# Eight buffers for parts of weights, each moved by 32 bytes more than the one before

## The chip, the cores and the metric

The program runs on one core of one Trainium2 chip. The metric is the device time of one execution in microseconds. The core's engines are TensorE (PE in the profile; its weight loads have a row of their own, PEld), VectorE (DVE), ScalarE (ACT), GpSimd (POOL) and SyncE (SP, which here issues the transfers).

## The reference

The program computes two layers of a decoder trunk on 512 positions of width 1024, in float32. Layer one is a gated short convolution followed by a feed-forward block with a convolution and a SiLU gate (inner width 2816). Layer two is an attention with forget gates (16 heads of 64) whose keys and values come from one shared projection, followed by a second feed-forward block of the same shape. Every block begins with an RMS norm and ends with an addition to the residual stream. Nearly all of the arithmetic is in the weight products:

```
proj = xn @ w_in                         # 1024 x 3072
x = x + (b * causal_dwconv(c * h)) @ w_out
kvf = h @ w_kvf;  qg = xn @ b_w_qg       # 1024 x 2064, 1024 x 2048
up = xn @ w_up                           # 1024 x 5632, in both layers
x = x + (silu(causal_dwconv(a)) * g) @ w_down   # 2816 x 1024, in both layers
```

## The kernel before

The residual stream lies transposed in SBUF as eight tiles of 128 features x 512 positions. Each float32 operand of a product is split into two parts, a high part (rounded to the matmul's float32r format) and a low part (the rest), and a product is made of three matmuls: high by high, high by low, low by high. The helper mac (L124 to L132) issues these three for each half of the 512 positions, so six matmuls of 256 columns for one block of 128 x 128 weights. In the order of its lines, L130 and L131 hold the high part of the weights as the stationary operand, L132 the low part. The moving operand is a tile of 2048 bytes per partition, read from its start (first half) or from 1024 bytes behind it (second half).

The weights come from HBM by SP's queue into wraw, three buffers of 128 x 1024 float32. The helper weights (L114 to L122) takes each buffer in pieces of up to 512 columns, and parts (L106 to L112) makes the two parts of a piece: ScalarE copies it into a whi buffer (L110), VectorE subtracts that from the piece into a wlo buffer (L111). A buffer holds four blocks of weights, at 0, 512, 1024 and 1536 bytes. There are four whi and four wlo buffers, used in turn; a buffer is free again when the last matmul that reads it is done. In the projection of the values (L368 to L404) the same buffers are filled in the same way but are the moving operand, and the activations are the stationary one.

The program gives addresses to its pools in the order in which they are opened (L58 to L65): const, big (58 tiles named g, which hold the activations' parts among others), sp (10 tiles s), ptp, misc, small, wraw, and last wsp with whi and wlo. All tiles from big to misc are 2048 bytes per partition, those of small are nine of 64 bytes, those of wraw 4096. So a whi or wlo buffer begins 576 bytes (nine times 64) behind a multiple of 2048 bytes counted from any g or s tile, the same for all eight of them. The addresses stand in no row of the trace; they follow from the tiles' sizes. The program's order on each engine is set by the order of its text and by the dependencies between tiles; no planner's cost enters it.

```
wraw = ctx.enter_context(tc.tile_pool(name="wraw", bufs=3))
wsp = ctx.enter_context(tc.tile_pool(name="wsp", bufs=4))
```

Of the kernel before, what the change touches and what calls it, by code (L numbers as in the profile page):

```python
# [15 lines left out]
F32 = mybir.dt.float32  # L16
F32R = mybir.dt.float32r
# [6 lines left out]
P = 128  # L24
T = 512
# [28 lines left out]
def trunk(ctx: ExitStack, tc: tile.TileContext, x_t, a_in, a_out, up0, down0, wk, wv, wf, wqg, b_out,  # L54
# [7 lines left out]
    misc = ctx.enter_context(tc.tile_pool(name="misc", bufs=8))  # L62
    small = ctx.enter_context(tc.tile_pool(name="small", bufs=3))
    wraw = ctx.enter_context(tc.tile_pool(name="wraw", bufs=3))
    wsp = ctx.enter_context(tc.tile_pool(name="wsp", bufs=4))  # L65
    banks = {n: ctx.enter_context(tc.tile_pool(name=n, bufs=b, space=PSUM))
             for n, b in (("mm", 2), ("st", 4), ("at", 2))}
    dram = ctx.enter_context(tc.tile_pool(name="dram", bufs=1, space=DRAM))
# [3 lines left out]
    def new(pool, tag, shape, dtype, **kw):  # L72
        count[0] += 1
        return pool.tile(shape, dtype, tag=tag, name=f"{tag}_{count[0]}", **kw)

    def G(dtype=F32):
        return new(big, "g", [P, T], dtype)

    def M(dtype=F32):
        return new(misc, "m", [P, T], dtype)  # L80
# [3 lines left out]
    def bank(name):  # L84
        return new(banks[name], name, [P, T], F32)
# [7 lines left out]
    pr = const.tile([P, NPAR], F32, tag="pr", name="pr")  # L93
    cs = const.tile([P, C_ET], F32, tag="cs", name="cs")
    x = [G() for _ in range(KT)]
    ones = const.tile([P, P], F32R, tag="ones", name="ones")
    nc.vector.memset(ones.bitcast(F32), 1.0)
    busy = G(F32R)
    nc.vector.memset(busy.bitcast(F32), 0.0)
    idle = bank("at")  # L100
# [4 lines left out]

    def parts(raw, n):  # L106

        hi = new(wsp, "whi", [P, T], F32R)
        lo = new(wsp, "wlo", [P, T], F32R)
        nc.scalar.copy(out=hi[:, :n], in_=raw)  # L110
        nc.vector.tensor_tensor(out=lo[:, :n], in0=raw, in1=hi[:, :n].bitcast(F32), op=ALU.subtract)  # L111
        return [(hi[:, c:c + P], lo[:, c:c + P]) for c in range(0, n, P)]  # L112

    def weights(src, nk=KT):  # L114

        cuts = [0, 8] if nk == 8 else [0, 8, 15, 22]
        for c0, c1 in zip(cuts[:-1], cuts[1:]):
            raw = new(wraw, "wraw", [P, 1024], F32)
            nc.sync.dma_start(out=raw[:, :(c1 - c0) * P], in_=src[:, c0 * P:c1 * P])
            for c in range(0, c1 - c0, 4):  # L120
                n = min(4, c1 - c0 - c) * P
                yield from parts(raw[:, c * P:c * P + n], n)  # L122

    def mac(ps, lh, rh, first, last):  # L124

        for h in range(2):

            f = slice(h * T // 2, (h + 1) * T // 2)
            go, end = first and h == 0, last and h == 1
            nc.tensor.matmul(ps[:, f], lhsT=lh[0], rhs=rh[0][:, f], start=go, stop=False, skip_group_check=True)  # L130
            nc.tensor.matmul(ps[:, f], lhsT=lh[0], rhs=rh[1][:, f], start=False, stop=False, skip_group_check=True)  # L131
            nc.tensor.matmul(ps[:, f], lhsT=lh[1], rhs=rh[0][:, f], start=False, stop=end, skip_group_check=True)  # L132
# [26 lines left out]
    def split(src, hi=None, lo=None, eng=None):  # L159
        hi = hi if hi is not None else G(F32R)  # L160
        lo = lo if lo is not None else G(F32R)
        nc.scalar.copy(out=hi, in_=src)  # L162
        (eng or nc.vector).tensor_tensor(out=lo, in0=src, in1=hi.bitcast(F32), op=ALU.subtract)  # L163
        return hi, lo
# [165 lines left out]
    def attention(norm, nxt_norm):  # L330
# [37 lines left out]
        for half in range(2):  # L368
            pv = [bank(n) for n in (("mm", "mm", "st", "st"), ("st", "st", "mm", "mm"))[half]]
            for u in range(4):  # L370
                raw = new(wraw, "wraw", [P, 1024], F32)
                nc.sync.dma_start(out=raw, in_=wv[half, u])
                w = []
                for c in (0, T):
                    hi = new(wsp, "whi", [P, T], F32R)
                    lo = new(wsp, "wlo", [P, T], F32R)
                    nc.scalar.copy(out=hi, in_=raw[:, c:c + T])
                    nc.vector.tensor_tensor(out=lo, in0=raw[:, c:c + T], in1=hi.bitcast(F32), op=ALU.subtract)
                    w.append((hi, lo))

                def step(t, k2):
                    k = 2 * u + k2
                    q = slice(t * P, (t + 1) * P)
                    mac(pv[t], (xkv[k][0][:, q], xkv[k][1][:, q]), w[k2], k == 0, k == KT - 1)

                if u < 3:
                    for k2 in range(2):
                        for t in range(NB):
                            step(t, k2)
                    if half == 0 and u == 1:  # L390
                        r, v1 = norm.finish()
                    if half == 0 and u == 2:

                        rt = const.tile([P, 16], F32, tag="rt", name="rt")[:, 0:NB]
                        tp = bank("st")
                        for i in range(NB):
                            nc.tensor.transpose(out=tp[:, i * H:(i + 1) * H], in_=r[:H, i * P:(i + 1) * P],
                                                identity=ident[:H, :H])
                        nc.vector.tensor_copy(out=rt, in_=tp[:, 0:NB * H].rearrange("p (i h) -> p i h", h=H)[:, :, 0])
                else:  # L400
                    for t in range(NB):
                        for k2 in range(2):
                            step(t, k2)
            for t in range(NB):  # L404
                for e in range(2):
                    v = G(F32R)
                    vs[t].append(v)
                    v = v.rearrange("p (c s d) -> p c s d", s=2, d=HD)
                    src = pv[t][:, e * 256:e * 256 + 256].rearrange("p (c d) -> p c d", d=HD)
                    nc.scalar.activation(out=v[:, :, e], in_=src, func=AF.Copy, scale=rt[:, t:t + 1])  # L410
                    nc.vector.scalar_tensor_tensor(out=v[:, :, 1 - e], in0=src, scalar=rt[:, t:t + 1],
                                                   in1=v[:, :, e].bitcast(F32), op0=ALU.mult, op1=ALU.subtract)
# [394 lines left out]
    ffn(up0, down0, PC_F[0], n2, n3, spill=True)  # L807
    n4 = Norm("ffn1")
    attention(n3, n4)
    ffn(up1, down1, PC_F[1], n4, None, last=True)  # L810

# [67 lines left out]
```

## Time and profile before

| | |
|---|---|
| median of 2 runs | 1233.8 us (1231.85 to 1235.76) |
| the profiled execution | 1233.1 us, of it 1231.3 us from the first to the last instruction |
| TensorE matmuls | 1216.5 us busy, 99% of the span, 10425 instructions |
| TensorE weight loads | 1189.0 us, 97%, 10425 instructions |
| VectorE, ScalarE, GpSimd | 678.6, 537.4, 203.1 us (55%, 44%, 16%) |
| TensorE's granted clock, mean | 0.996 |
| transfers | 124.14 MB, mean 101 GB/s |

Matmuls are pipelined: the 276 ns shown for one of 256 columns is its way from start to end, and several are under way at once. What the stream of them costs is read from the distance between their starts, so from counts over a stretch of time, or from the first and the last start of an unbroken run.

### The profile page before, as it was taken

What the parts mean: (1) busy time and instruction counts of PE and PEld (TensorE: products, weight loads), DVE (VectorE), ACT (ScalarE), POOL (GpSimd) and SP (SyncE); (2) the same over time, 40 slices, a digit from 0 to 9 for tenths busy, and PEclk for the clock granted to TensorE, in tenths of its full rate; (3) what the DMA queues carried; (4) which work ended last, traced back from release to release, by engine and by line L of the source; (5) the groups of instructions that cost most, each with busy time, mean ns of one, the idle gap of its engine ahead of it and who ended that gap; (6) DMA issues with size and microseconds to landing.
All of it is one profiled execution on the core that took longest, in us unless ns stands there. A gap on an engine that the chain in (4) does not pass through costs nothing.

```text
span 1231.3 us, 24568 instructions
## 1 busy us (share of the span) xinstructions
PE 1216.5 (99%) x10425; PEld 1189.0 (97%) x10425; DVE 678.6 (55%) x1163; ACT 537.4 (44%) x973; POOL 203.1 (16%) x181
## 2 busy tenths in 40 slices
PE   9999999999999999999999899999999999999998
PEld 8999999999999999999998788889999999999998
DVE  6755556555555533344646787876565555553222
ACT  5433345334333433333556767775543334342221
POOL 0100021111111100000123435442111111110000
PEclk9999999999999999999999999999999999999999
DMA  6233233333333344342342212124233233233341
GB/s 215 87 103 101 88 104 92 97 104 93 97 104 91 93 130 125 121 140 87 95 139 79 84 52 86 53 87 129 86 104 101 89 103 101 89 99 104 116 119 45
DMA packets 39374, 124.14 MB, mean 101 GB/s; under 512 B 4384, under 2 KB 4896, under 8 KB 39264
## 3 DMA queue, kind: packets, MB, share of 16 engines
q1 hardware_dynamic: 38048, 120.41, 31.8%
q10 hardware_dynamic: 1152, 1.97, 0.5%
q8 instruction: 81, 1.33, 0.4%
q14 instruction: 29, 0.24, 0.1%
q0 software_dynamic: 64, 0.20, 0.0%
HBM read 118.33 MB, written 4.23 MB: 100 GB/s over the span
## 4 chain that ended last, share of the span: by engine, by line
PE 90%; ACT 4%; DVE 3%; POOL 2%; issue 1%; DMA 0%; SPq 0%; DVEq 0%; POOLq 0%; ACTq 0%
PE st L131 18%; PE st L130 17%; PE st L132 17%; PE mm L130 11%; PE mm L132 11%; PE mm L131 11%; ACT s L189 1%; PE st L620 1%; PE at L658 1%; PE st L649 1%; POOL m L667 1%; DVE s L624 1%; DVE wlo L111 1%; ACT g L189 1%; ACT g L162 1%
## 5 line engine op out<-in xcount | busy, mean ns | idle before, releaser
L130 PE MATMUL st<-g,whi 128*128 128x256 f32 x1686 | 465.5, 276 | 0.0
L131 PE MATMUL st<-g,whi 128*128 128x256 f32 x1686 | 465.4, 276 | 0.0
L132 PE MATMUL st<-g,wlo 128*128 128x256 f32 x1686 | 465.4, 276 | 0.0
L110 ACT CAST whi<-wraw 128x512 fp32r<-128x512 f32 (+1 forms) x394 | 240.4, 611 | 473.6 <-PE st L131 291.9
L111 DVE TENSOR_TENSOR wlo<-wraw,whi 128x512 fp32r<-128x512 f32 (+1 forms) x394 | 283.6, 720 | 222.9 <-ACT whi L110 218.3
L130 PE MATMUL mm<-g,whi 128*128 128x256 f32 x1242 | 346.2, 279 | 0.0
L131 PE MATMUL mm<-g,whi 128*128 128x256 f32 x1242 | 343.5, 277 | 0.0
L132 PE MATMUL mm<-g,wlo 128*128 128x256 f32 x1242 | 343.5, 277 | 0.0
L130 PEld LDWEIGHTS st<-g,whi 128*128 128x128 f32 x1686 | 316.6, 188 | 0.1
L131 PEld LDWEIGHTS st<-g,whi 128*128 128x128 f32 x1686 | 316.5, 188 | 0.1
L132 PEld LDWEIGHTS st<-g,wlo 128*128 128x128 f32 x1686 | 316.5, 188 | 0.0
L130 PEld LDWEIGHTS mm<-g,whi 128*128 128x128 f32 x1242 | 233.5, 188 | 1.8
L131 PEld LDWEIGHTS mm<-g,whi 128*128 128x128 f32 x1242 | 233.4, 188 | 1.3
L132 PEld LDWEIGHTS mm<-g,wlo 128*128 128x128 f32 x1242 | 233.2, 188 | 0.1
L323 POOL TENSOR_TENSOR m<-m,m 128x512 f32<-128x512 f32 x44 | 69.1, 1573 | 408.3 <-DVE m L322 370.9
L162 ACT CAST g<-m 128x512 fp32r<-128x512 f32 x66 | 40.8, 619 | 90.4 <-POOL m L323 66.8
L163 DVE TENSOR_TENSOR g<-m,g 128x512 fp32r<-128x512 f32 x51 | 36.8, 722 | 67.3 <-ACT g L162 66.7
L224 POOL TENSOR_TENSOR m<-m,m 128x512 f32<-128x512 f32 x21 | 27.9, 1330 | 175.5 <-ACT m L222 153.6
L640 POOL TENSOR_SCALAR s<-s,sm 128x128 f32<-128x128 f32 (+3 forms) x64 | 41.4, 660 | 75.5 <-DVE sm L637 69.2
L189 ACT ACTIVATE s<-s,bb 128x128 f32<-128x128 f32 (+3 forms) x64 | 35.4, 555 | 22.9 <-DVE bb L633 22.8
L241 ACT ACTIVATE m<-m,pr 128x512 f32<-128x512 f32 x52 | 37.7, 725 | 15.9 <-DVE m L316 13.0
L242 DVE SCALAR_TENSOR_TENSOR m<-m,pr,m 128x511 f32<-128x511 f32 x52 | 39.0, 750 | 9.5 <-ACT m L241 9.5
(170 smaller groups left out, 1312.3 us busy)
## 6 DMA issues: line engine op xcount, KB each, us to landing
wraw<-up SPq DMA_DIRECT2D x88, 512.0 KB, 3.5
wraw<-down SPq DMA_DIRECT2D x32, 448.0 KB, 3.5
wraw<-a_in SPq DMA_DIRECT2D x21, 512.0 KB, 3.6
wraw<-down SPq DMA_DIRECT2D x16, 512.0 KB, 3.5
wraw<-wqg SPq DMA_DIRECT2D x16, 512.0 KB, 3.6
wraw<-a_out SPq DMA_DIRECT2D x8, 512.0 KB, 3.5
ld<-xsp SPq DMA_DIRECT2D x16, 256.0 KB, 2.8
wraw<-wv SPq DMA_DIRECT2D x8, 512.0 KB, 3.6
```

The source lines that it names most:

```text
L110: nc.scalar.copy(out=hi[:, :n], in_=raw)
L111: nc.vector.tensor_tensor(out=lo[:, :n], in0=raw, in1=hi[:, :n].bitcast(F32), op=ALU.subtract)
L130: nc.tensor.matmul(ps[:, f], lhsT=lh[0], rhs=rh[0][:, f], start=go, stop=False, skip_group_check=True)
L131: nc.tensor.matmul(ps[:, f], lhsT=lh[0], rhs=rh[1][:, f], start=False, stop=False, skip_group_check=True)
L132: nc.tensor.matmul(ps[:, f], lhsT=lh[1], rhs=rh[0][:, f], start=False, stop=end, skip_group_check=True)
L162: nc.scalar.copy(out=hi, in_=src)
L163: (eng or nc.vector).tensor_tensor(out=lo, in0=src, in1=hi.bitcast(F32), op=ALU.subtract)
L189: chain["exp"] = ordered(nc.scalar.activation(**kw), chain["set"])
L241: nc.scalar.activation(out=y, in_=src, func=AF.Copy, scale=pr[:, col + 2:col + 3])
L242: nc.vector.scalar_tensor_tensor(out=y[:, 1:T], in0=src[:, 0:T - 1], scalar=pr[:, col + 1:col + 2], in1=y[:, 1:T], op0=ALU.mult, op1=ALU.add)
L323: nc.gpsimd.tensor_tensor(out=g, in0=g, in1=y, op=ALU.mult)
L640: nc.gpsimd.tensor_scalar(out=s, in0=s, scalar1=sm[:, e:e + 1], scalar2=1.0, op0=ALU.mult, op1=ALU.mult)
```

## The change

The pool wsp is replaced by two, whip for the four whi buffers and wlop for the four wlo buffers. Ahead of them a pool with one tile of 32 bytes per partition (pad0), which nothing writes or reads, is put behind wraw. Each buffer is allocated with 520 columns, 2080 bytes, of which the first 512 columns are used as before. A helper WP hands out a pair. Counted from a g tile, modulo 2048 bytes, the four whi buffers then begin at 608, 640, 672 and 704, the four wlo buffers at 736, 768, 800 and 832. The instructions and their order in the text are the same.

```diff
-    wsp = ctx.enter_context(tc.tile_pool(name="wsp", bufs=4))
+    ctx.enter_context(tc.tile_pool(name="pad0", bufs=1)).tile([P, 8], F32, tag="pad0", name="pad0")
+    whip = ctx.enter_context(tc.tile_pool(name="whip", bufs=4))
+    wlop = ctx.enter_context(tc.tile_pool(name="wlop", bufs=4))
...
+    def WP():
+
+        hi = new(whip, "whi", [P, T + 8], F32R)[:, 0:T]
+        return hi, new(wlop, "wlo", [P, T + 8], F32R)[:, 0:T]
...
     def parts(raw, n):
-        hi = new(wsp, "whi", [P, T], F32R)
-        lo = new(wsp, "wlo", [P, T], F32R)
+        hi, lo = WP()
...
                 for c in (0, T):
-                    hi = new(wsp, "whi", [P, T], F32R)
-                    lo = new(wsp, "wlo", [P, T], F32R)
+                    hi, lo = WP()
```

## Rows read from the trace of the kernel before

**Rows 1.** The page's part 1: TensorE's busy time, share, instructions.
```profile
PE 1216.5 (99%) x10425; PEld 1189.0 (97%) x10425; DVE 678.6 (55%) x1163; ACT 537.4 (44%) x973; POOL 203.1 (16%) x181
```

**Rows 2.** The page's part 4: the chain that ended last, by engine.
```profile
PE 90%; ACT 4%; DVE 3%; POOL 2%; issue 1%; DMA 0%; SPq 0%; DVEq 0%; POOLq 0%; ACTq 0%
```

**Rows 3.** Groups of instructions by line and shape: count, busy us, mean ns, idle before.
```profile
L130 PE MATMUL st<-g,whi 128*128 128x256 f32 x1686 | 465.5, 276 | 0.0
...
L130 PE MATMUL mm<-g,whi 128*128 128x256 f32 x1242 | 346.2, 279 | 0.0
...
L130 PE MATMUL st<-s,whi 128*128 128x256 f32 x110 | 30.4, 276 | 0.0
...
L130 PE MATMUL mm<-whi,g 128*128 128x256 f32 x64 | 18.1, 282 | 0.0
```

**Rows 4.** Waits of TensorE, two of ten rows: total us, times, longest.
```profile
PE st L620 <- DVE mx L624: 3.4, 1, 3.4
...
PE mm L130 <- ACT g L162: 0.6, 1, 0.6
```

**Rows 5.** Windows, TensorE alone: length, busy (count), granted clock, DMA share, GB/s.
```profile
33.00:193.00 160.00, 160.00 (x1414) 1.00 0.31 96
200.00:540.00 340.00, 340.00 (x3003) 1.00 0.35 105
...
840.00:1190.00 350.00, 350.00 (x3088) 1.00 0.35 105
```

**Rows 6.** Timeline of TensorE, first stage: start us, duration us, instruction.
```profile
13.06 0.28 PE L130 MATMUL mm<-g,g 128*128 128x256 f32 x1
...
25.54 0.28 PE L132 MATMUL st<-g,g 128*128 128x256 f32 x1
25.65 0.28 PE L130 MATMUL st<-g,whi 128*128 128x256 f32 x1
...
31.19 0.28 PE L132 MATMUL st<-g,wlo 128*128 128x256 f32 x1
```

**Rows 7.** Timeline of TensorE, the projection of the values.
```profile
543.61 0.28 PE L130 MATMUL mm<-whi,g 128*128 128x256 f32 x1
...
544.29 0.28 PE L130 MATMUL st<-whi,g 128*128 128x256 f32 x1
...
544.56 0.39 PE L130 MATMUL mm<-whi,g 128*128 128x256 f32 x1
...
545.02 0.28 PE L130 MATMUL mm<-whi,g 128*128 128x256 f32 x1
...
554.44 0.28 PE L131 MATMUL st<-wlo,g 128*128 128x256 f32 x1
```

**Rows 8.** Timeline of TensorE, the keys' projection.
```profile
593.66 0.28 PE L130 MATMUL mm<-g,whi 128*128 128x256 f32 x1
...
605.44 0.28 PE L131 MATMUL mm<-g,whi 128*128 128x256 f32 x1
...
609.20 0.28 PE L130 MATMUL mm<-g,whi 128*128 128x256 f32 x1
...
609.54 0.28 PE L130 MATMUL mm<-g,whi 128*128 128x256 f32 x1
```

**Rows 9.** Timeline of TensorE: two matmuls of 512 columns with 16 columns of weights.
```profile
623.73 0.39 PE L506 MATMUL at<-m,E 128*16 128x512 f32 x1
623.96 0.40 PE L507 MATMUL at<-m,E 128*16 128x512 f32 x1
```

**Rows 10.** Groups of ScalarE and VectorE: count, busy us, mean ns, idle before and releasers.
```profile
L111 DVE TENSOR_TENSOR wlo<-wraw,whi 128x512 fp32r<-128x512 f32 x362 | 265.9, 735 | 192.7 <-ACT whi L110 188.1 <-PE st L131 2.0 <-PE mm L131 2.0
...
L110 ACT CAST whi<-wraw 128x512 fp32r<-128x512 f32 x362 | 224.0, 620 | 418.8 <-PE st L131 254.8 <-PE mm L131 134.3 <-ACT m L222 10.6
...
L242 DVE SCALAR_TENSOR_TENSOR m<-m,pr,m 128x511 f32<-128x511 f32 x52 | 39.0, 750 | 9.5 <-ACT m L241 9.5
...
L169 DVE SCALAR_TENSOR_TENSOR g<-g,pr,g 128x512 fp32r<-128x512 f32 x32 | 23.6, 750 | 4.8 <-ACT g L168 4.7
```

## Prediction

> **What bounds the kernel now.** I read the engines' busy times first: TensorE fills 99% of the span [rows 1], and the chain of waits lies on it for 90% [rows 2]. The groups by line come next: matmuls that load a whi or wlo buffer as weights are, over L130, L131 and L132, 3 x (1686 + 1242 + 110) = 9,114 of 10,425, and those that stream one are 6 x 64 = 384 [rows 3]. The idle time ahead of them is nothing. TensorE's list of waits says the same from the other side: its longest wait is 3.4 us, once, in the attention, and among its ten rows none is for the copy or the subtraction that fills these buffers [rows 4]. So neither filling nor freeing the buffers sets the end; the distance from one matmul's start to the next does, and only through it can an address count.
>
> That distance is read from counts. In three long windows, which hold 7,505 matmuls, it is 113.2 to 113.3 ns, at a granted clock of 1.00 [rows 5]; at that level (2.4 GHz) 256 columns are 106.7 ns by themselves. But the same shape also runs at other distances. In the first stage, where weights and moving tiles are both g tiles, 104 steps take 12.48 us, 120.0 ns each; the next matmuls load whi and wlo, and with no pause between the two 47 steps take 5.54 us, 117.9 ns each [rows 6]. That is the one place where a change of buffer alone goes with a change of pace, so the profile doesn't rule out that addresses matter. Two other places show what else matters. The values' projection begins at 113.3 ns (six steps in 0.68 us), is held up once, and then runs at 117.8 ns (80 steps in 9.42 us) with the same kinds of operands at the same distances from each other [rows 7]. The keys' projection runs at 117.8 ns (100 steps in 11.78 us) with g and whi, and after a hold-up at 113.3 ns with the same two [rows 8]. So there are several paces, a hold-up can switch between them at equal addresses, and the fast one has most of the time.
>
> **The change part by part.** It adds no instruction and no wait. The tile of 32 bytes is never written or read. The pools ahead of it keep their addresses, so SP's transfers into wraw land where they did, in the same order. whi and wlo had four buffers each and still have, freed by the same last matmuls; one pool or two makes no difference to who waits for whom. All this is 0, and nothing covers it, because nothing is issued.
>
> The copies and subtractions write to, and partly read from, buffers that begin at odd multiples of 32 bytes. No copy of before writes to such a place. The nearest row is VectorE's work in the convolution, whose operands begin one column (4 bytes) off: 750 ns for 511 columns, the same as 750 ns for 512 columns that begin on a tile's start [rows 10]. I take 0. If each copy took twice its 620 ns, the idle time ahead of it, 418.8 us over 362 copies or 1.16 us each, nearly all of it waiting for TensorE to free a buffer, would hold the added 0.62 us; the subtraction, 735 ns, has 0.53 us of idle ahead of it [rows 10]. What would be late next, were that cover gone, is the matmul at the head of a new buffer; today none waits.
>
> What is left is the reading by TensorE. Before, every weight block stood 576 bytes, modulo 512 thus 64, from the moving tile's grid. After, the eight buffers stand at 96, 128, 160, 192 (high) and 224, 256, 288, 320 (low) modulo 512; four of the eight, one in two in each kind, are at an odd multiple of 32 bytes, which no operand of before is. Bounds: from above, every one of the 9,114 at the 120.0 ns of the g tiles [rows 3, 6], 9,114 x 6.7 = 61 us more. From below, every one at the bare 106.7 ns, 9,114 x 6.6 = 60 us less. In between, the stretches now at 117.8 with whi or wlo (48 in the first stage, some 101 in the keys, the 384 of the values) go to 113.3: 533 x 4.5 = 2.4 us less [rows 6 to 8].
>
> I take 0, by the long windows. They run through four blocks in each of eight buffers, and through both halves of the moving tile. Counted modulo 2048 the weights there lie 64, 576, 1088 and 1600 bytes from the moving tile, and the pace is the same to 0.1 ns over 340 us [rows 5]. The first six steps of the values, where the two operands change places (the distance is then minus 64), keep it too [rows 7]. And the 6.6 ns over the bare columns aren't the weights': two matmuls of 512 columns with 16 columns of weights start 0.23 us apart, about twice 113.3, where a load eight times smaller should have given most of the excess back [rows 9].
>
> The Trainium skill speaks here as well: "SBUF — State Buffer", section "Who interferes with whom", says that contention arises only at the port pair that VectorE and GpSimd share, and that TensorE waits for nobody at SBUF. By it the change is worth 0 whatever the offsets. The trace agrees in the long windows, but equal shapes at 113.3, 117.8 and 120.0 ns are something that the section doesn't explain, so I don't take it as proof.
>
> The sum is 0 against the profiled execution's own 1233.1 us (a span of 1231.3 and 1.8 around it), which lies 0.7 under the median of the two runs, 1233.8. I forecast 1233.5 us; this case by itself reaches from 1230.7 (the 2.4 us given back) to 1240 (a few thousand steps in the slower pace).
>
> **Rivals.** *Slower: odd buffers load worse.* Place: each block in a buffer at an odd multiple of 32 bytes, half of the 9,114. Price: at 120.0 ns, 4,557 x 6.7 = 30.5 us, so 1264 us; at 117.8 ns, 4,557 x 4.5 = 20.5 us, 1254. It is decided by whether these loads cost 5.4 ns or more each, since 2% of 1233 is 24.7 us; if all eight buffers pay, 2.7 ns suffice, and the two prices become 41 and 61 us (1274 and 1294). For it: the step from 120.0 to 117.9 at a change of buffer, and that no row has such an offset. Against it: four distances modulo 2048 at one pace. Chance 0.20.
>
> *Slower within the measurement: the pace after a hold-up falls otherwise.* If one of the two feed-forward blocks stayed at 117.8 ns throughout, the windows' counts say what that costs: 1414 + 3003 of them 19.9 us, 3088 of them 13.9 us. Against it: in the windows of both blocks the fast pace holds through every change of buffer [rows 5]. By its price it ends as no change; chance 0.08.
>
> *Faster: the distance of 64 bytes is itself a bad one.* Then spread offsets would take off part of the 6.6 ns; half of it is 30 us, 1203 us, all of it 60 us, 1173. Against it are the two matmuls with small weights. The Trainium skill, "TensorE: Matmul & The Clock Gate", section "Back-to-back issue gap", gives N/2.4 + 2.5 ns, an estimate of 109.2 ns for 256 columns, which would make it 1196 us; the trace has no such step at 256 columns in float32. Chance 0.10.
>
> *The change does not do what it says.* If addresses were rounded up to 64 bytes, the offsets would be multiples of 64 as before, and the time the same. No row shows an address, so the trace speaks neither way. Chance 0.05.
>
> **The numbers.** No change 0.70, of it 0.08 for the pace that falls otherwise and 0.05 for rounded addresses; slower by over 2% 0.20; faster by over 2% 0.10. 2% is about what a measurement of this kernel can tell from no change. The range runs from 1228 to 1264: it holds the forecast's case and the slower case at the price of half the buffers, and leaves out the faster case and the slower one with all buffers.
>
> **What would show it.** Right: windows inside the two feed-forward blocks of the changed kernel hold 1414, 3003 and 3088 matmuls again within two or three. Slower: within such a window the distances of the starts change from one buffer to the next, every 24 matmuls, and with the odd ones longer. A pace that a hold-up chose would change only at hold-ups. Faster: counts above 3,030 in the window of 340 us. I would be wrong in kind if TensorE had waits for the copy at L110 or the subtraction at L111.

## The result, and the profile after

The changed kernel took 1272.11 us (median of two runs, 1271.87 to 1272.35) against 1233.8 before: a ratio of 1.031, 95% interval 1.024 to 1.0381. It is slower, and the forecast of no change and its range (up to 1264) were both wrong.

The page of the changed kernel, part 1, and its three longest waits of TensorE (total us, times, longest):

```profile
PE 1255.6 (99%) x10425; PEld 1228.4 (97%) x10425; DVE 676.8 (53%) x1163; ACT 537.9 (42%) x973; POOL 202.5 (16%) x181
```

```profile
PE st L626 <- DVE mx L630: 3.3, 1, 3.3
PE at L772 <- DVE g L107: 1.6, 1, 1.6
PE at L664 <- ACT pt L169: 1.4, 3, 1.0
```

TensorE issues the same 10,425 matmuls and fills 99% of a span that is 38.8 us longer (1270.1 against 1231.3). It waits for nothing new: neither the copies (now L117) nor the subtractions (L118) are among its waits, as in [rows 4]. The subtraction is no slower than in [rows 10], and has no less idle time ahead of it; the group of the changed kernel:

```profile
L118 DVE TENSOR_TENSOR wlo<-wraw,whi 128x512 fp32r<-128x512 f32 x362 | 263.5, 728 | 211.2 <-ACT whi L117 210.8
```

So the time is in the distance between matmul starts. The windows of [rows 5], in the changed kernel (length, busy and count, granted clock, DMA share, GB/s):

```profile
33.00:193.00 160.00, 160.00 (x1358) 1.00 0.30 94
200.00:540.00 340.00, 340.00 (x2876) 1.00 0.33 101
840.00:1190.00 350.00, 349.93 (x2952) 1.00 0.31 96
```

The granted clock is 1.00 as before, and 340 us hold 2876 matmuls instead of 3003: 118.2 ns each instead of 113.2. In the two others it is 117.8 and 118.6 ns; the third window also takes in some of the attention here, which ends later than before. All three stages pay: the values' projection starts at 564.3 us, 20.7 later than in [rows 7]; the first matmul of its group shows that:

```profile
L137 PE MATMUL mm<-whi,g x64: 276/281/387, 564.3 to 610.5; 128*128 128x256 f32 x64
```

The rest of the 38.8 us, 18.1, comes behind that point: 1.3 up to the unbroken run of matmuls that begins with the attention's output projection (at 834.01 us before, at 856.04 after), and 16.8 in that run and the second feed-forward block. Inside a window the distance isn't even. The rows below are the first matmul of each of five buffers that follow one another (24 matmuls each), from the timeline of the changed kernel's TensorE. Which buffer a block stands in follows from the program's order, not from a row; the pools hand out their four buffers in the order first, fourth, third, second. Here it is the pair at distances 128 and 256 (high, low part; bytes modulo 512 from the moving tile's grid), then 96 and 224, then 192 and 320, then 160 and 288.

```profile
238.16 0.28 PE L137 MATMUL st<-g,whi 128*128 128x256 f32 x1
...
241.02 0.28 PE L137 MATMUL mm<-g,whi 128*128 128x256 f32 x1
...
243.86 0.28 PE L137 MATMUL mm<-g,whi 128*128 128x256 f32 x1
...
246.59 0.28 PE L137 MATMUL mm<-g,whi 128*128 128x256 f32 x1
...
249.50 0.28 PE L137 MATMUL mm<-g,whi 128*128 128x256 f32 x1
```

The four pairs take 2.86, 2.84, 2.73 and 2.91 us. Twenty-four matmuls at 113.3 ns would be 2.72: the pair at 192 and 320 runs at the old pace, the three others at 118 to 121 ns. Two of the slow pairs begin at odd multiples of 32 bytes, but one of them, at 128 and 256, does not, so that the rival of the odd buffers cannot be the whole of it.

### The profile page after: what moved, and what is told of

Read it like the earlier page. It is cut to its first block, busy times and chain, and to the rows that moved or that the text cites. A ratio compares the mean times of both kernels' runs of the same rounds, so it can differ in the third digit from the quotient of the medians.

```text
span 1270.1 us, 24568 instructions
## 1 busy us (share of the span) xinstructions
PE 1255.6 (99%) x10425; PEld 1228.4 (97%) x10425; DVE 676.8 (53%) x1163; ACT 537.9 (42%) x973; POOL 202.5 (16%) x181
## 4 chain that ended last, share of the span: by engine, by line
PE 91%; ACT 4%; DVE 3%; POOL 2%; issue 1%; DMA 0%; SPq 0%; DVEq 0%; POOLq 0%; ACTq 0%
PE st L139 18%; PE st L138 18%; PE st L137 18%; PE mm L138 11%; PE mm L137 11%; PE mm L139 11%; ACT s L196 1%; PE st L626 1%; PE at L664 1%; PE st L655 1%; POOL m L673 1%; DVE s L630 1%; ACT g L196 1%; ACT g L169 1%; DVE wlo L118 0%
## 5 line engine op out<-in xcount | busy, mean ns | idle before, releaser
L138 PE MATMUL st<-g,whi 128*128 128x256 f32 x1686 | 473.9, 281 | 0.0
L139 PE MATMUL st<-g,wlo 128*128 128x256 f32 x1686 | 473.6, 281 | 0.0
L137 PE MATMUL st<-g,whi 128*128 128x256 f32 x1686 | 472.7, 280 | 0.0
L117 ACT CAST whi<-wraw 128x512 fp32r<-128x512 f32 (+1 forms) x394 | 240.3, 611 | 513.5 <-PE st L138 313.5
L118 DVE TENSOR_TENSOR wlo<-wraw,whi 128x512 fp32r<-128x512 f32 (+1 forms) x394 | 281.3, 714 | 243.4 <-ACT whi L117 242.9
L137 PE MATMUL mm<-g,whi 128*128 128x256 f32 x1242 | 350.8, 282 | 0.0
L138 PE MATMUL mm<-g,whi 128*128 128x256 f32 x1242 | 349.1, 281 | 0.0
L139 PE MATMUL mm<-g,wlo 128*128 128x256 f32 x1242 | 348.8, 281 | 0.0
```

## The experiments

The theories tried first: A, the pace hangs on the distance modulo 128 between the weights and the moving tile, and only 64 allows 113.3 ns; B, it costs that neighbouring buffers, or the high and the low part, differ; C, odd multiples of 32 bytes cost, and an even buffer between them suffers. Every experiment but the last changes addresses alone. The pads are tiles that nothing touches, as in the change. The distances named are those of the weights from the moving tile modulo 256, worked out from the tiles' sizes. Each experiment but the last was timed in one execution, beside one or more of the kernel before; fifteen of the kernel before lie between 1231.3 and 1236.5 us, and the losses below are of 28 us and more.

**All eight buffers moved together, or spread by 128 bytes.**

```diff
-    wsp = ctx.enter_context(tc.tile_pool(name="wsp", bufs=4))
+    ctx.enter_context(tc.tile_pool(name="pad0", bufs=1)).tile([P, 16], F32, tag="pad0", name="pad0")
+    wsp = ctx.enter_context(tc.tile_pool(name="wsp", bufs=4))
```

That is u64; u32, u128, u256 and u384 have [P, 8], [P, 32], [P, 64] and [P, 96]. In s128 there is no pad, and the buffers are longer:

```diff
-        hi = new(wsp, "whi", [P, T], F32R)
-        lo = new(wsp, "wlo", [P, T], F32R)
+        hi = new(wsp, "whi", [P, T + 32], F32R)[:, 0:T]
+        lo = new(wsp, "wlo", [P, T + 32], F32R)[:, 0:T]
```

u64, expected: 

> The kernel before with a pad of 64 bytes ahead of its eight buffers: all eight stand 640 bytes (modulo 128: 0) behind the moving tiles' grid instead of 576 (modulo 128: 64), and none differs from another. Theory A (the pace hangs on the distance of the weights from the moving tile modulo 128 bytes, and only 64 allows 113.3 ns): slow, 117.8 to 120 ns in the long windows, 1274 to 1294 us. Theory B (what costs is that one buffer differs from the next, or the high from the low part): 113.3 ns, 1233 us. Theory C (odd multiples of 32 bytes cost, and the even buffer between them suffers from its neighbours): 113.3 ns, 1233 us.

u32, expected: 

> A pad of 32 bytes ahead of the eight buffers, which do not differ from one another: distance 96 modulo 128 for all. Theory A: slow, about the 118.4 ns that the buffer at this distance has in the changed kernel, 1233 + 9114 x 5.1 ns = 1280 us. Theory B: 113.3 ns, 1233 us. Theory C: slow, all eight are odd, 1274 to 1294 us.

u128, expected: 

> A pad of 128 bytes ahead of the eight buffers: distance 704, which is 64 modulo 128 but no longer 64 modulo 512. Theories A, B and C: 113.3 ns, 1233 us. Were the one distance of before special (modulo 256 or 512): slow, over 1254 us.

s128, expected: 

> No pad, but each buffer 128 bytes longer, so that the eight differ by 128 bytes from one to the next: all distances differ, and all are 64 modulo 128. Theory A: 113.3 ns, 1233 us. Theory B: slow, like the changed kernel, about 1272 us. Theory C: 1233 us.

Measured, beside the kernel before at 1233.09 us: u64 1280.14, u32 1266.79, u128 1267.75, s128 1233.85. The window from 200 to 540 us of the four, in this order, a fence each:

```profile
200.00:540.00 340.00, 340.00 (x2865) 1.00 0.32 99
```

```profile
200.00:540.00 340.00, 340.00 (x2898) 1.00 0.33 102
```

```profile
200.00:540.00 340.00, 340.00 (x2887) 1.00 0.33 101
```

```profile
200.00:540.00 340.00, 340.00 (x3002) 1.00 0.34 105
```

That is 118.7, 117.3, 117.8 and 113.3 ns. B falls twice over: buffers that all stand alike are slow (u64, u32), and eight that differ are not (s128). C falls with u64, where nothing is odd and which is the slowest. A has the direction right on three of four (u32 was forecast at 1280 us and took 1266.79) and missed u128: all eight at 192, which is 64 modulo 128, are slow, although half of the pairs in s128 stand at 192 too and are fast. The trace of u128 says more. Starts of TensorE in its first stage:

```profile
24.54 0.28 PE L130 MATMUL st<-g,whi 128*128 128x256 f32 x1
...
29.87 0.28 PE L132 MATMUL st<-g,wlo 128*128 128x256 f32 x1
29.98 0.39 PE L230 MATMUL at<-m,ones 128*128 128x512 f32 x1
30.20 0.39 PE L231 MATMUL at<-m,ones 128*128 128x512 f32 x1
30.43 0.28 PE L130 MATMUL st<-g,whi 128*128 128x256 f32 x1
...
31.26 0.28 PE L131 MATMUL st<-g,whi 128*128 128x256 f32 x1
```

The first 47 steps take 5.33 us, 113.4 ns each. Then come the norm's two matmuls of 512 columns, and behind them seven steps take 0.83 us, 118.6 ns at the rows' resolution; the window above says that it stays at 117.8. In the kernel before, the same two matmuls stand between 117.9 ns in [rows 6] and the 113.3 of [rows 5]: the mirror image. So at 64 modulo 128 there are two paces, and the stream changes from one to the other at an interruption.

The other distances have two paces as well, closer together. In u64 the window ahead of the norm's two matmuls at 204.81 us holds

```profile
33.00:193.00 160.00, 160.00 (x1336) 1.00 0.30 93
```

which is 119.8 ns, and behind them the window above has 118.7, all at distance 128. In u32 the 394 steps from the first to the second of these rows take 46.76 us, 118.7 ns each; the norm's matmuls follow, and then 117.3 ns again:

```profile
853.33 0.28 PE L131 MATMUL st<-g,whi 128*128 128x256 f32 x1
...
900.09 0.28 PE L132 MATMUL mm<-g,wlo 128*128 128x256 f32 x1
```

Neither comes near 113.3 at either of its paces. The next four runs ask what the choice hangs on, whether it is the distance or the address that counts, and what a mixture does.

u256, expected: 

> All eight buffers 256 bytes further than before: distance 320 modulo 512, which is 64 modulo 256 as before. The run with 128 bytes more (distance 192) ran at 117.8 ns throughout, the one with buffers 128 bytes apart at 113.3. Theory A2 (distances of 64 modulo 128 allow both paces, and modulo 256 decides which one a hold-up leaves behind: 64 the fast, 192 the slow): 113.3 ns, 1233 us. Theory A3 (which of the two paces stays is incidental to each program): either, 1233 or 1268 us. Theory D (any move of all eight away from the distance of before is slow): 1267 to 1280 us.

u384, expected: 

> All eight buffers 384 bytes further: distance 448 modulo 512, which is 192 modulo 256. Theory A2: 117.8 ns, 1268 us. Theory A3: either. Theory D: slow.

**Moving tiles and weights moved together** (all64), by a pad ahead of big:

```diff
-    big = ctx.enter_context(tc.tile_pool(name="big", bufs=58))
+    ctx.enter_context(tc.tile_pool(name="padb", bufs=1)).tile([P, 16], F32, tag="padb", name="padb")
+    big = ctx.enter_context(tc.tile_pool(name="big", bufs=58))
```

Expected: 

> A pad of 64 bytes ahead of the pool big: the moving tiles and the eight buffers all begin 64 bytes further, their distance stays 576. If the distance counts: 113.3 ns in the long windows, 1233 us. If the weights' own address counts (it is now that of the run with a pad of 64 ahead of the buffers): 118 to 120 ns, 1280 us.

**High and low parts at different distances** (lo64; lo128 has [P, 32]; parts and the values' loop take from the two pools):

```diff
-    wsp = ctx.enter_context(tc.tile_pool(name="wsp", bufs=4))
+    whip = ctx.enter_context(tc.tile_pool(name="whip", bufs=4))
+    ctx.enter_context(tc.tile_pool(name="pad0", bufs=1)).tile([P, 16], F32, tag="pad0", name="pad0")
+    wlop = ctx.enter_context(tc.tile_pool(name="wlop", bufs=4))
```

lo64, expected: 

> The four buffers of high parts as before (distance 64 modulo 128), those of low parts 64 bytes further (distance 0 modulo 128). If each load pays by itself, the one in three that loads a low part costs the 5.5 ns more of the run with all at that distance: 9114 / 3 x 5.5 = 17 us, 1250 us. If one bad load in three takes the fast pace from all: 1266 to 1280 us.

Measured, beside the kernel before at 1233.46: u256 1237.22, u384 1267.94, all64 1234.05, lo64 1274.05. The same window, in this order:

```profile
200.00:540.00 340.00, 340.00 (x3002) 1.00 0.34 106
```

```profile
200.00:540.00 340.00, 340.00 (x2888) 1.00 0.32 101
```

```profile
200.00:540.00 340.00, 340.00 (x3002) 1.00 0.34 105
```

```profile
200.00:540.00 340.00, 340.00 (x2876) 1.00 0.32 101
```

A2 has both of its forecasts: 64 modulo 256 fast (113.3 ns), 192 slow (117.7 ns). Two runs alone would not exclude A3, under which either could have come out so; the later runs bear on that. That u256 is 3.8 us over its neighbour lies outside the long windows; its mean granted clock was 0.994, and four executions of the kernel before at 0.994 took 1234.4 to 1236.5 us, so the distance need not be the cause. In all64 the weights have the very address of u64, and it runs at 113.3 ns: the distance counts, not the address. Which of the two paces it has can differ even so, at the same distance: 47 steps of the keys' projection take 5.33 us in the kernel before and 5.53 in all64, 113.4 and 117.7 ns each.

```profile
612.38 0.28 PE L130 MATMUL mm<-g,whi 128*128 128x256 f32 x1
...
617.71 0.28 PE L132 MATMUL mm<-g,wlo 128*128 128x256 f32 x1
```

```profile
612.72 0.28 PE L130 MATMUL mm<-g,whi 128*128 128x256 f32 x1
...
618.25 0.28 PE L132 MATMUL mm<-g,wlo 128*128 128x256 f32 x1
```

In lo64 one load in three stands at 128, and the mean is 118.2 ns, not the 115.1 of the first reading: within a block, one bad load in three costs nearly as much as three (118.7 in u64).

**Pairs 64 bytes apart, and high and low at 64 and 192.** s64 is s128 with T + 16.

s64, expected: 

> Each buffer 64 bytes longer, no pad: the four pairs of buffers stand at distances 64, 128, 192 and 0 modulo 256, high and low part of a pair alike. All start at multiples of 64 bytes. If only the matmuls that load from a buffer at 128 or 0 pay, and the pace comes back at once in the others: half of 9114 x 5.5 ns (the price in the run with all at 128) = 25 us, 1258 us, with 113.3 ns inside the blocks of the pairs at 64 and 192. If a bad buffer takes the pace from its good neighbours: 1268 to 1280 us. If the odd multiples of 32 were the cause: 1233 us.

lo128, expected: 

> High parts at distance 64 modulo 256 as before, low parts at 192: both 64 modulo 128, so that every block mixes the two. If mixing the two distances frees the pace as in the run with buffers 128 bytes apart: 113.3 ns in the long windows, 1233 us. If the loads at 192 hold the slow pace that they had alone: 117.8 ns, 1268 us.

Measured, beside the kernel before at 1232.62 (median of 15): s64 1260.78, lo128 1232.7. For s64 the first matmul of five buffers that follow one another, from its timeline (the pairs at 64, 0, 192 and 128, by the program's order), and for lo128 the window:

```profile
241.01 0.28 PE L130 MATMUL mm<-g,whi 128*128 128x256 f32 x1
...
243.74 0.28 PE L130 MATMUL mm<-g,whi 128*128 128x256 f32 x1
...
246.62 0.28 PE L130 MATMUL mm<-g,whi 128*128 128x256 f32 x1
...
249.35 0.28 PE L130 MATMUL mm<-g,whi 128*128 128x256 f32 x1
...
252.19 0.28 PE L130 MATMUL st<-g,whi 128*128 128x256 f32 x1
```

```profile
200.00:540.00 340.00, 340.00 (x3002) 1.00 0.34 105
```

The pairs take 2.73, 2.88, 2.73 and 2.84 us: 113.8, 120.0, 113.8 and 118.3 ns. Each pair pays by itself, and in this stretch the fast pace comes back within a buffer's first matmuls; half of them slow is the first reading, which forecast 1258 us. The pair at 0 runs at the 120.0 ns that the first stage has in [rows 6], where both operands are g tiles and the distance is 0 too; the number alone doesn't tell 0 from 128, since u64 has about 120 as well in its window from 33 to 193 us. Mixing 64 and 192 inside each block, in lo128, gives the fast pace.

**The rule put to use** (v192): the values' parts go into the pt tiles, moved so that the stationary g tiles stand at 64 from them; whi and wlo get a pad of 64 to stay at 64.

```diff
+    ctx.enter_context(tc.tile_pool(name="padp", bufs=1)).tile([P, 48], F32, tag="padp", name="padp")
     ptp = ctx.enter_context(tc.tile_pool(name="ptp", bufs=6))
...
-                    hi = new(wsp, "whi", [P, T], F32R)
-                    lo = new(wsp, "wlo", [P, T], F32R)
+                    hi = new(ptp, "pt", [P, T], F32R)
+                    lo = new(ptp, "pt", [P, T], F32R)
```

Expected: 

> The rule that weights should stand 64 bytes modulo 256 behind the moving tile, used where the kernel before breaks it: the parts of the values' weights, which are moving operands there, go into the pt tiles, moved 192 bytes from the grid of g, so that the stationary g tiles stand at 64; the same puts the products with the probabilities at 64. whi and wlo go to 320, which is 64 as before. By the rule: the 384 matmuls of the values at 113.3 instead of 117.8 ns, 1.7 us, and about half a microsecond in the attention: 1231.5 us, ratio 0.998. If a hold-up decides at these places whatever the distance: no change, 1233 to 1234 us. Three pairs of buffers instead of four could hold TensorE up: slower by some microseconds.

Measured over five rounds: 1235.14 against 1232.62 us, ratio 1.0016, 95% interval 1.0004 to 1.0028. It didn't gain. Two windows of the values' projection and two on either side of the norm's matmuls at about 880 us, in v192. A count takes in the matmuls that began up to 0.28 us ahead of the window, which matters in windows as short as these: the pace is 9.28, 32.28 and 38.28 us over the count.

```profile
545.00:554.00 9.00, 9.00 (x82) 1.00 0.46 148
555.00:587.00 32.00, 32.00 (x273) 1.00 0.38 125
```

```profile
840.00:878.00 38.00, 38.00 (x325) 1.00 0.40 132
882.00:920.00 38.00, 38.00 (x338) 1.00 0.32 98
```

The values run at the fast pace (113.2 ns) for 9 us and lose it at a hold-up (118.2); and the attention's output projection, with the first two products of the second feed-forward block, runs at the slow pace (117.8) and the stream finds the fast one (113.3) behind the norm's matmuls, all at distance 64. So a distance of 64 makes the fast pace possible and, in the long unbroken runs of this kernel, likely; it doesn't secure it, and A2 holds as a tendency only. No version here beats the kernel before.

## Why the prediction was wrong

The parts that it set to 0 were 0: no instruction, wait or transfer was added, and neither the copies (619 ns) nor the subtractions (728 ns) slowed down. That the whole effect could only come through the distance between matmul starts was right, and so was the reading that more than one pace exists at one distance.

The step that failed is "I take 0, by the long windows": it put the price of TensorE's reading at other addresses at nothing, and the changed kernel paid 118.2 ns for 113.2 in the middle window, 38.8 us over the span. The prediction counted the distances 64, 576, 1088 and 1600 modulo 2048 as four samples at one pace. The runs show a pace that goes by the distance modulo 256, and in that the four are one: blocks lie 512 bytes apart and the halves of a moving tile 1024. The long windows held a single sample, the good one. One sample at a distance other than 64 modulo 128 was in the trace, the first stage at 0 with 120.0 ns [rows 6]. The prediction named it as "the one place where a change of buffer alone goes with a change of pace" and then took it as a point for the odd buffers only; the pair of s64 at 0 repeats it. The values at 192 and the keys at 64, which also ran at 117.8 ns [rows 7, 8], it rightly put down to hold-ups: 113.4 ns was seen at 192 as well (u128, first stage) and 117.8 at 64 (v192). What it missed is that a hold-up chooses only among the paces that a distance has, and that 113.3 ns was seen only where the distance is 64 modulo 128.

The rival on the slower side had the wrong cause. Odd multiples of 32 bytes are slow (u32, 117.3 ns), but 128 is slower (118.7 ns). Its price was that of half the buffers, and the range stopped there. Three pairs of four stand badly, and in a bad pair both parts pay: 118.2 ns in the middle window is 5.0 ns over 113.2, and 9,114 times that is 45.6 us. The 38.8 measured is less, since some stretches were at 117.8 ns already and one stretch of the attention, which holds some 620 of these loads, took no longer (157.0 us from 676.99 us on, 156.2 in the changed kernel from 699.85 on). The line "if all eight buffers pay" gave 1274 us at 117.8 ns, close to the 1272 measured, but for another reason; that is luck. The place that would show it was named: distances that change from one buffer to the next, every 24 matmuls, are what the timeline shows, with the fast pair the one at 192 and 320. The count of 9,114 leaves out three groups like this one of the kernel before; with them it is 9,264, and no price in the prediction moves by more than 1 us:

```profile
L130 PE MATMUL mm<-s,whi 128*128 128x256 f32 x50 | 13.8, 276 | 0.0
```

The rule of the Trainium skill cited there ("SBUF — State Buffer", "Who interferes with whom"), by which TensorE waits for nobody at SBUF, was not taken as proof, and yet the forecast agreed with it. The measurements decide: with both operands TensorE's own, a move of 64 bytes of one of them costs 5.4 ns per matmul here (u64, 118.7 against 113.3 in the window from 200 to 540 us).

The rivals of a faster pace and of rounded addresses find no support: no long window of any run is below 113.2 ns, and pads of 32 and 64 bytes act differently.

## What to carry to other kernels

Where TensorE streams back to back, a pad or a new tile ahead of a pool of weights can move the whole kernel by some per cent with no new wait and the same instructions; count matmuls in a long window before and after any change of layout. When samples seem to show that an address doesn't matter, first work out in which modulus they differ. Here a distance of 64 bytes modulo 128 between the stationary and the moving operand, with 64 modulo 256 among the buffers, kept 113.3 ns for 256 columns in the long windows; spreading buffers by multiples of 128 cost nothing (s128).

## What the hardware showed

The distances modulo 256 and the pace in the window from 200 to 540 us, worked out from its counts: 64: 113.2 to 113.3 ns (the kernel before, u256, all64); 64 mixed with 192: 113.3 (s128, lo128); 96: 117.3 (u32); 192 alone: 117.7 to 117.8 (u128, u384); 128: 118.7 (u64); 0: 120.0 (one pair of s64, and, outside that window, [rows 6]). Outside that window other paces were seen at the same distances: 117.8 at 64 (v192), 113.4 at 192 (u128), 118.7 at 96 (u32) and 119.8 at 128 (u64). The granted clock was 1.00 in all of these windows. What within TensorE makes the distance count, and what in a hold-up chooses between the paces, no run shows; distances between these, at multiples of 4 or 16 bytes, were not tried.
